# Planner rates, later SSM phase tables and a half output stage in two equal parts, in a fused conformer and SSM step

## The chip, the core and the metric

The kernel runs on one core of a Trainium2 chip. The metric is the device time of one launch in microseconds (us); the median of three runs of the kernel before is 1973.45 us. The engines of the core work side by side and wait for each other by semaphores: TensorE (PE, matrix products, with PEld its weight loads), VectorE (DVE), ScalarE (ACT), GpSimd (POOL), and SyncE (SP), whose queue issues the DMAs.

## The reference

One step of a decoder layer on 2048 prompt tokens and 8 sample tokens, width 1024, all in fp32. A gated causal convolution of 31 taps and a diagonal complex SSM (32 groups of 16 channels and 64 states) run side by side, are merged, projected, and an input embedding is added under a gate. Cut to what matters (only the prompt's names, without the states that are returned):

```
h = rmsnorm(x, g_pre)
proj = h @ w_in                       # 1024 -> c_a, c_b, c_z (1024 each), s_x, s_z (512 each), g_c, g_s (1024 each)
u = c_a * sigmoid(c_b)
v = causal_depthwise_conv(u, 31 taps)
v = silu(layernorm(v)) * silu(c_z)    # mean and variance over the 1024 channels
y_c = v @ w_pc
lb = exp(a*dt) (complex), bb = (lb-1)/a * b
s[t] = lb * s[t-1] + bb @ s_x[t];  ys = Re(c @ s) + d * s_x
ys = gelu(ys); ys = ys * sigmoid(ys @ w_glu + b_glu) * silu(s_z)
m = sigmoid(g_c) * y_c + sigmoid(g_s) * (ys @ w_ps)
x1 = x + rmsnorm(m @ w_out, g_post)
y = x1 + rmsnorm(p @ w_ple, g_ple) * sigmoid(x1 @ w_pg + b_pg)
```

## The kernel before

Channels lie on the 128 partitions and tokens on the free axis. The tokens are worked in two halves: the first has 1032 (1024 of the prompt and the 8 samples), in three blocks of 344; the second 1024, in two of 512. Every matrix product is made of three fp32r products, hi by hi, hi by lo and lo by hi (L288 to L290): operands are split into a rounded part (hh, vh, mh, whi: ScalarE, L338 and L251) and the rest (hl, vl, ml, wlo: VectorE or GpSimd, L331). A weight block is 128 x 1024 (raw, 512 KB). It is fetched by SP's queue into one of two buffers, ScalarE casts it to whi, GpSimd subtracts to wlo in two pieces of 512, and only then is the buffer free again.

One half runs through these stages: the input norm; s_x; the pairs c_b and c_a (u in unit c); g_c; s_z; the SSM's products and w_glu; g_s with w_ps; c_z; w_pc (tiles vh, vl); w_out (tiles mh, ml of m); w_pg (mh, ml of x1). Beside them VectorE runs the convolution, 31 multiply-adds per channel block with the accumulator in PSUM (L183, acc and u), of which some taps are taken by ScalarE and GpSimd instead (cq and ca). Then the LayerNorm: the mean by a product with a matrix of averages (L363 and L364, nh and nl), u minus mean, the squares, the variance by the same product, an inverse square root, and v = silu(...) times cz, split into vh and vl. Before the first SSM product the kernel makes tables in `ssm_setup`: for each of four channel batches b, gt (powers times bb), its transposes on TensorE (L609) and products with c (L619); and the phases rho and ph, which undo and redo the rotation of the complex state so that only a real decay is left to scan. They come in two lots, x = 0 for batches 0 and 1, and x = 1 for 2 and 3, each by doubling from 1 to 128 columns (`spar` and `ph` tiles, L177 and L180).

What is computed is fixed; the order is made by a planner when the kernel is built. Tasks are Python generators that yield the engine and the earliest time of the next piece. `Background` (L24 on) holds a clock for VectorE, ScalarE and GpSimd and one for TensorE; each `stage` adds the cost of its products to TensorE's clock and `pump` lets those tasks go on whose planned time has come. `cV`, `cS`, `cG` give the planned cost of n columns on each engine, `use` adds it, `pick` chooses VectorE or GpSimd. A task that wants TensorE (a "P" task: the transposes, the SSM's and the means' products) goes only when it has been ready for a margin of 1.2 us. Each engine then runs its instructions strictly in the order so made. `room(k)` holds a task until k SBUF units are free. PSUM gives six banks to products (`bank`).

In the output stage of the first half the tokens go in two parts, a with the block of 344 and b with the two others, 688: w_out a, w_out b, w_pg a, w_pg b; each part fetches and splits its weights anew. The norm of o, x1 and the outputs (y tasks: e, sgp) of a part are VectorE operations of 344 or 688 columns. In the same time `next_h` brings in the second half's x (xn) and makes its hh and hl.

## Time and profile before

| what | value |
|---|---|
| three runs | 1972.57, 1973.45, 1979.47 us |
| profiled execution | 1971.99 us, span 1970.2 us |
| TensorE busy | 1918.5 us (97%), 10386 products |
| VectorE busy | 1442.1 us (73%) |
| ScalarE, GpSimd busy | 765.6 us (39%), 784.8 us (40%) |
| TensorE's granted clock, mean | 0.989 |
| chain that ended last | TensorE 85%, issue 4%, VectorE 4%, GpSimd 2% |

The profile is of one execution. Busy times of an engine are shares of the whole span and say little of a stage; what a stage waits for is read from the waits, and where a moment is disputed from the timeline of one engine, whose rows give start, duration, engine, line, operation, output and inputs, and in brackets how long the engine sat idle before and what released it. TensorE's products overlap, so the pace is the distance from one start to the next, or a window's time over its number of products.

### The profile page before, as it was taken

The numbers are of one execution on the slowest core, as the hardware profiler recorded it, in microseconds if no ns is written. First come the engines' busy times: TensorE is split into PE (matmuls) and PEld (weight loads), VectorE is DVE, ScalarE is ACT, GpSimd is POOL, SyncE is SP. The second block draws the span as 40 slices with busy tenths as digits, with TensorE's granted clock in tenths as the row PEclk, the third lists the DMA queues.
The fourth block names the chain that finished last, engine by engine and source line by source line (L and its number), as shares of the span: only waits on it lengthen the run. The fifth ranks groups of instructions, "written<-read, shape, count | busy, mean of one in ns | idle before, by whom it ended". The sixth has DMA issues, their size and how long they took to land.

```text
span 1970.2 us, 26641 instructions
## 1 busy us (share of the span) xinstructions
PE 1918.5 (97%) x10386; PEld 1723.0 (87%) x10386; DVE 1442.1 (73%) x1696; ACT 765.6 (39%) x1276; POOL 784.8 (40%) x573
## 2 busy tenths in 40 slices
PE   8897999999999999999899999999999999999998
PEld 7797999999999999999798788888888888888877
DVE  6889997899899876444884479888589843442686
ACT  7424211227311364254532223444731353223542
POOL 1437623315422223253533222687743222224554
PEclk9998999999999999999899999999999999999999
DMA  8461344542122215342554463212212211422455
GB/s 315 155 203 62 100 133 141 177 144 78 51 83 78 102 50 193 116 142 93 190 197 164 172 200 123 74 60 91 71 48 75 97 67 43 160 107 77 148 189 174
DMA packets 103286, 243.58 MB, mean 124 GB/s; under 512 B 11752, under 2 KB 44648, under 8 KB 103144
## 3 DMA queue, kind: packets, MB, share of 16 engines
q1 hardware_dynamic: 102840, 241.68, 36.2%
q8 instruction: 81, 1.33, 0.3%
q14 instruction: 45, 0.37, 0.1%
q10 hardware_dynamic: 320, 0.20, 0.0%
HBM read 188.17 MB, written 54.62 MB: 123 GB/s over the span
## 4 chain that ended last, share of the span: by engine, by line
PE 85%; issue 4%; DVE 4%; POOL 2%; ACT 1%; DMA 1%; POOLq 0%; ACTq 0%; SPq 0%; DVEq 0%
PE bank L288 27%; PE bank L290 26%; PE bank L289 26%; PE bank L774 2%; POOL wlo L331 1%; PE bank L777 1%; PE bank L719 1%; DMA raw<-in_w 1%; POOL ca L331 1%; DVE sgp L331 1%; DVE o L183 0%; DVE o L331 0%; DVE ml L331 0%; DVE spar L183 0%; PE bank L308 0%
## 5 line engine op out<-in xcount | busy, mean ns | idle before, releaser
L331 POOL TENSOR_TENSOR wlo<-raw,whi 128x512 fp32r<-128x512 f32 x386 | 566.5, 1486 | 1082.2 <-ACT whi L251 1064.5
L288 PE MATMUL bank<-hh,whi 128*128 128x344 f32 (+1 forms) x1888 | 665.9, 353 | 0.9 <-ACT whi L251 0.9
L289 PE MATMUL bank<-hl,whi 128*128 128x344 f32 (+1 forms) x1888 | 659.9, 350 | 6.8 <-DVE hl L331 6.8
L290 PE MATMUL bank<-hh,wlo 128*128 128x344 f32 (+1 forms) x1888 | 661.2, 350 | 1.4 <-POOL wlo L331 1.4
L183 DVE SCALAR_TENSOR_TENSOR acc<-u,prm,acc 128x1024 f32<-128x1024 f32 x412 | 530.5, 1288 | 11.2
L289 PEld LDWEIGHTS bank<-hl,whi 128*128 128x128 f32 x1888 | 356.9, 189 | 39.4 <-DVE hl L331 7.1
L288 PEld LDWEIGHTS bank<-hh,whi 128*128 128x128 f32 x1888 | 356.4, 189 | 36.9 <-ACT whi L251 1.5
L290 PEld LDWEIGHTS bank<-hh,wlo 128*128 128x128 f32 x1888 | 356.8, 189 | 35.6 <-POOL wlo L331 2.4
L251 ACT CAST whi<-raw 128x512 fp32r<-128x512 f32 x388 | 223.9, 619 | 148.5 <-PE bank L289 68.6
L288 PE MATMUL bank<-mh,whi 128*128 128x344 f32 (+1 forms) x640 | 227.4, 355 | 7.7 <-ACT whi L251 5.8
L290 PE MATMUL bank<-mh,wlo 128*128 128x344 f32 (+1 forms) x640 | 227.1, 355 | 5.2 <-POOL wlo L331 5.1
L289 PE MATMUL bank<-ml,whi 128*128 128x344 f32 (+1 forms) x640 | 226.6, 354 | 0.3 <-DVE ml L331 0.3
L331 POOL TENSOR_TENSOR ca<-ca,cq 128x512 f32<-128x512 f32 x104 | 132.2, 1300 | 39.5 <-ACT cq L881 36.1
L288 PEld LDWEIGHTS bank<-mh,whi 128*128 128x128 f32 x640 | 122.6, 192 | 20.8 <-ACT whi L251 7.1
L290 PEld LDWEIGHTS bank<-mh,wlo 128*128 128x128 f32 x640 | 122.7, 192 | 18.9 <-POOL wlo L331 7.8
L289 PEld LDWEIGHTS bank<-ml,whi 128*128 128x128 f32 x640 | 122.5, 191 | 12.3 <-DVE ml L331 1.1
L289 PE MATMUL bank<-vl,whi 128*128 128x344 f32 (+1 forms) x320 | 111.9, 350 | 0.7 <-DVE vl L331 0.7
L288 PE MATMUL bank<-vh,whi 128*128 128x344 f32 (+1 forms) x320 | 112.2, 351 | 0.0
L290 PE MATMUL bank<-vh,wlo 128*128 128x344 f32 (+1 forms) x320 | 112.0, 350 | 0.0
L881 ACT ACTIVATE cq<-u,prm 128x512 f32<-128x512 f32 x104 | 73.4, 722 | 55.0 <-POOL ca L331 45.9
L331 DVE TENSOR_TENSOR oacc<-oacc,sq 128x344 f32<-128x344 f32 (+1 forms) x35 | 30.6, 874 | 79.2 <-ACT sq L1388 78.7
L177 DVE TENSOR_TENSOR gcl<-bank,gcl 128x344 f32<-128x344 f32 (+1 forms) x40 | 23.5, 587 | 65.7 <-PE bank L290 65.7
(213 smaller groups left out, 2447.7 us busy)
## 6 DMA issues: line engine op xcount, KB each, us to landing
raw<-in_w SPq DMA_DIRECT2D x194, 512.0 KB
cq<-cq SPq DMA_DIRECT2D x12, 512.0 KB
e<-e SPq DMA_DIRECT2D x8, 516.0 KB
rt<-e SPq DMA_DIRECT2D x8, 516.0 KB
gc<-gc SPq DMA_DIRECT2D x8, 516.0 KB
m<-gs SPq DMA_DIRECT2D x8, 516.0 KB
gcl<-gc SPq DMA_DIRECT2D x8, 516.0 KB
m2l<-m SPq DMA_DIRECT2D x8, 516.0 KB
```

The lines of the kernel that those rows point to most:

```text
L177: V.tensor_tensor(out=out, in0=a, in1=b, op=op)
L183: V.scalar_tensor_tensor(out=out, in0=a, scalar=s, in1=b, op0=op0, op1=op1)
L251: S.copy(out=hi, in_=t[:, c])
L288: T.matmul(o, hi[:, w], rh[:, c0:c0 + n], start=kt == 0, stop=False)
L289: T.matmul(o, hi[:, w], rl[:, c0:c0 + n], start=False, stop=False)
L290: T.matmul(o, lo[:, w], rh[:, c0:c0 + n], start=False, stop=kt == k - 1)
L331: (V if e == "V" else GP).tensor_tensor(out=out, in0=a, in1=b, op=op)
L719: T.matmul(pvs[rr][half_[i], jj], we[:, g * P + rr * 64:g * P + rr * 64 + 64], U[:, g, 8:8 + ne], start=True, stop=True)
L774: T.matmul(pvs[i][:, jj], TW[:, :, 2 * j + i], U[:, 2 * j + i, o0:136], start=True, stop=False)
L777: T.matmul(pvs[i][:, jj], cq[half_[i], x * 512 + j * P:x * 512 + (j + 1) * P], X[half_[i], x, j, o0:136], start=False, stop=x == 1)
L881: S.activation(out=q[:, h], in_=u[:, k + x * 512:k + x * 512 + 512], func=AF.Identity, scale=w(k))
```

## The change

Four things. The planner's rates: n/930 + 0.1 for VectorE in place of n/960 + 0.08, n/1190 for n/1250 on ScalarE, 0.3 for 0.16 of fixed cost on GpSimd, 0.4375 ns a column and 7 ns for a product of TensorE in place of n/2400 and 3 ns, `pick` to match, and larger costs for the table work. The margin of P tasks is 4.0 us, not 1.2. The phase tables: rho and x = 0 are made after table b = 0, x = 1 after b = 2, and `ssm_batch` fetches its phases only when they are there. The output stage of the first half has two parts of 516 tokens, each in two blocks of 258. Besides, the gelu and ysn tasks wait for one or two free units.

```diff
-                at = max(self.clock[e], r) if e in self.clock else r + (1.2 if e == "P" else 0.0)
+                at = max(self.clock[e], r) if e in self.clock else r + (4.0 if e == "P" else 0.0)
...
-        return "V" if v + n / 960.0 <= g + n / 478.0 + 0.3 else "G"
+        return "V" if v + n / 930.0 <= g + n / 478.0 + 0.4 else "G"
...
-    cV = lambda n: 0.08 + n / 960.0
+    cV = lambda n: 0.1 + n / 930.0
...
-    cS = lambda n: 0.13 + n / 1250.0
-    cG = lambda n: 0.16 + n / 478.0
+    cS = lambda n: 0.13 + n / 1190.0
+    cG = lambda n: 0.3 + n / 478.0
+    cPr = lambda n: 0.007 + n * 0.4375e-3
...
+        OUT_PARTS = [[[(0, 258), (258, 258)], [(516, 258), (774, 258)]], [[(0, 512)], [(512, 512)]]]
...
-                bg.pe += 3 * k * (n / 2400.0 + 0.003)
+                bg.pe += 3 * k * cPr(n)
...
-            r0 = use("V", 5.6, 3.0)
+            r0 = use("V", 11.0, 3.0)
...
-            tt(k1, mag, mag)
...
-            tt(rho, k1, k1)
...
-                unit_length(*ph[0], v2)
...
-            r0 = use("V", 6.5, r0)
-            for x in range(2):
+            def phases(x, r0):
...
-                    r0 = use("V", 2.0 + 6 * cV(4 * m), r0)
+                    r0 = use("V", 4.0 + 6 * m / 120.0, r0)
...
+                tables["phases"] = 2 * x + 2
+                tables["ph", x] = queue["data"] + 1.0
+                return r0
...
+                if b == 0:
...
+                    tt(k1, mag, mag)
...
+                    tt(rho, k1, k1)
...
+                        unit_length(*ph[0], v2)
...
+                    r0 = use("V", 13.0, r0)
+                if b % 2 == 0:
+                    r0 = yield from phases(b // 2, r0)
...
-            phu = alloc(name="sph")
-            rp = dma(out=phu[:, 0:1024], in_=ph_d[b], after=tables[b])
...
-            r = max(r1, rp)
+            while tables["phases"] < b + 1:
+                yield None, bg.now + 1.0
+            yield from room(3)
+            phu = alloc(name="sph")
+            r = max(r1, dma(out=phu[:, 0:1024], in_=ph_d[b], after=tables["ph", b // 2]))
...
+                yield from room(1)
...
+                yield from room(1)
...
-            parts = [[blocks[i] for i in p] for p in PARTS[h]]
+            parts = OUT_PARTS[h]
```

The steps of rho (from `tt(k1, mag, mag)` on) and `phases` stand in `ssm_setup`; `phu`, the tile of the phases, in `ssm_batch`; `room(1)` in `gelu_task`. The lines of the new kernel are numbered 1 to 18 higher (products L290 to L292, transposes L591, means L365 and L366).

First place: TensorE, the first transposes of the table of batch 0 (ident, gt) in the pairs of c_b and c_a. Before, where 720 products with h stand ahead of them:

```order
L288 MATMUL bank<-hh_431,whi 128x344
L289 MATMUL bank<-hl_432,whi 128x344
L290 MATMUL bank<-hh_431,wlo 128x344
L609 MATMUL bank<-ident,gt_2027 128x128 x4
L288 MATMUL bank<-hh_417,whi 128x344
```

Now, with 336 ahead of them:

```order
L290 MATMUL bank<-hh_436,whi 128x344
L291 MATMUL bank<-hl_437,whi 128x344
L292 MATMUL bank<-hh_436,wlo 128x344
L591 MATMUL bank<-ident,gt_1264 128x128 x4
L290 MATMUL bank<-hh_422,whi 128x344
```

The transposes have moved 384 products towards the start.

Second place: VectorE, behind the products that end bb (which gt needs). Before, rho begins here, and gt of batch 0 stands about 200 rows on, behind both lots of phases:

```order
L177 TENSOR_TENSOR bb_729<-bb_729 128x256
L331 TENSOR_TENSOR re_743<-re_743,rt_989 128x1032
L331 TENSOR_TENSOR re_743<-re_743,rt_1102 128x1032
L177 TENSOR_TENSOR spar_727<-spar_727 128x16 x2
L177 TENSOR_TENSOR rho<-spar_727 128x16
```

Now gt is made here, and rho stands behind the first tile of u and the first operation of its convolution (acc<-u,prm):

```order
L178 TENSOR_TENSOR bb_737<-bb_737 128x256
L333 TENSOR_TENSOR re_744<-re_744,rt_989 128x1032
L178 TENSOR_TENSOR gw_1265<-pwr_120,bb_737 128x512
L178 TENSOR_TENSOR gw_1265<-pwr_121,bb_737 128x512
L178 TENSOR_TENSOR gt_1264<-gw_1265 128x512
...
L178 TENSOR_TENSOR u_1379<-bank,sg_1275 128x344 x2
L839 MEMSET u_1379 128x30
...
L181 TENSOR_SCALAR acc<-u_1379,prm 128x1024
L178 TENSOR_TENSOR spar_735<-spar_735 128x16 x2
L178 TENSOR_TENSOR rho<-spar_735 128x16
```

The table goes ahead of the phases, and the phases of x = 0 go behind the work that u brings.

Third place: TensorE, the product that gives the variance (nh, nl with avgr) and the first products of v. Before, 264 products with h stand between them:

```order
L364 MATMUL bank<-nl_6807,avgr 128x344
L288 MATMUL bank<-hh_417,whi 128x344
...
L290 MATMUL bank<-hh_431,wlo 128x344
L288 MATMUL bank<-vh_7014,whi 128x344
L289 MATMUL bank<-vl_7015,whi 128x344
```

Now 120 do:

```order
L366 MATMUL bank<-nl_7010,avgr 128x344
L290 MATMUL bank<-hh_422,whi 128x344
...
L292 MATMUL bank<-hh_436,wlo 128x344
L290 MATMUL bank<-vh_7217,whi 128x344
L291 MATMUL bank<-vl_7218,whi 128x344
```

The mean that comes before the variance has moved by the same 144 products, with 192 products between the two as before.

## Rows read from the trace of the kernel before

**Rows 1.** The page's part 1: busy time, share of the span, instructions.

```profile
PE 1918.5 (97%) x10386; PEld 1723.0 (87%) x10386; DVE 1442.1 (73%) x1696; ACT 765.6 (39%) x1276; POOL 784.8 (40%) x573
```

**Rows 2.** Timeline of TensorE: start, duration, product, count, and in brackets idle before.

```profile
84.09 0.65 PE L289 MATMUL bank<-hl,whi 128*128 128x344 f32 x1 [6.78 <-DVE hl L331]
...
196.17 1.09 PE L609 MATMUL bank<-ident,gt 128*128 128x128 f32 x4 [14.08 <-issue]
```

**Rows 3.** Timeline of VectorE, 105 to 197.

```profile
105.22 0.71 DVE L177 TENSOR_TENSOR spar<-spar 128x16 f32<-128x16 f32 x2
...
192.17 0.69 DVE L177 TENSOR_TENSOR ph<-ph 128x512 f32<-128x512 f32 x1
...
194.06 1.29 DVE L177 TENSOR_TENSOR gw<-pwr,bb 128x512 f32<-128x512 f32 x2
195.38 0.69 DVE L177 TENSOR_TENSOR gt<-gw 128x512 f32<-128x512 f32 x1
```

**Rows 4.** Windows: length, PE, PEld, DVE, ACT, POOL busy (instructions), clock, DMA share, GB/s.

```profile
97.70:142.00 44.30, 44.30 (x282) 44.30 (x282) 36.79 (x136) 13.93 (x26) 19.34 (x25) 1.00 0.63 194
142.00:193.00 51.00, 40.09 (x255) 39.81 (x253) 49.56 (x96) 21.61 (x34) 35.04 (x27) 0.92 0.22 73
193.00:520.00 327.00, 323.41 (x2134) 315.68 (x2135) 298.07 (x340) 106.47 (x200) 118.76 (x89) 0.99 0.38 125
520.00:667.30 147.30, 147.30 (x936) 147.30 (x935) 135.47 (x142) 32.50 (x60) 38.31 (x28) 1.00 0.25 86
```

**Rows 5.** VectorE's groups by form, busy and mean ns: 114.6:141.6, then 152.3:186.6.

```profile
L177 DVE TENSOR_TENSOR ph<-ph,spar 128x8 f32<-128x8 f32 x14 | 2.7, 240 | 0.2
...
L177 DVE TENSOR_TENSOR ph<-ph,spar 128x8 f32<-128x8 f32 x6 | 3.9, 692 | 0.1
```

**Rows 6.** Timeline of GpSimd, 152 to 160.

```profile
152.31 7.58 POOL L331 TENSOR_TENSOR ca<-ca,cq 128x512 f32<-128x512 f32 x6 [0.62 <-ACT cq L881]
```

**Rows 7.** Waits of VectorE, 219 to 668: total us, times, longest.

```profile
DVE u L177 <- PE bank L290: 10.4, 6, 3.0
DVE gs L177 <- PE bank L290: 6.4, 14, 1.6
```

**Rows 8.** Timelines of VectorE, ScalarE and TensorE, 666 to 756.

```profile
666.14 1.28 DVE L183 SCALAR_TENSOR_TENSOR u<-u,prm,acc 128x1024 f32<-128x1024 f32 x1
...
709.61 1.42 ACT L376 ACTIVATE mean<-bank,epsc 128x344 f32<-128x344 f32 x3
...
714.55 1.23 DVE L177 TENSOR_TENSOR acc<-acc,mean 128x1032 f32<-128x1032 f32 x1 [9.14 <-ACT acc L384]
...
754.64 1.23 DVE L331 TENSOR_TENSOR vl<-cz,vh 128x1032 fp32r<-128x1032 f32 x1 [1.12 <-ACT vh L338]
...
755.93 0.43 PE L289 MATMUL bank<-vl,whi 128*128 128x344 f32 x1 [0.71 <-DVE vl L331]
```

**Rows 9.** Windows at the start of w_pg in the first half.

```profile
936.00:978.00 42.00, 35.49 (x200) 33.20 (x199) 32.48 (x32) 23.02 (x37) 22.06 (x14) 0.92 0.56 194
978.00:996.00 18.00, 13.68 (x51) 12.59 (x52) 16.95 (x22) 4.75 (x9) 7.10 (x4) 0.62 0.58 188
```

**Rows 10.** Waits of TensorE, 930 to 1060: total us, times, longest.

```profile
PE bank L288 <- ACT whi L251: 5.3, 3, 3.9
PE bank L290 <- POOL wlo L331: 3.3, 3, 1.7
```

**Rows 11.** Timeline of VectorE, 987 to 990.

```profile
987.58 1.66 DVE L331 TENSOR_TENSOR ml<-o,mh 128x688 fp32r<-128x688 f32 x2 [0.83 <-ACT mh L338]
```

**Rows 12.** A window of products of 512 columns.

```profile
1640.00:1700.00 60.00, 60.00 (x260) 48.57 (x259) 19.88 (x12) 17.37 (x26) 17.29 (x12) 1.00 0.23 79
```

**Rows 13.** Timeline of TensorE, 207 to 209.

```profile
207.24 1.87 PE L619 MATMUL bank<-cbd,gt 128*128 128x32 f32 x16
208.94 0.40 PE L288 MATMUL bank<-hh,whi 128*128 128x344 f32 x1
```

**Rows 14.** Timeline of VectorE, 1061 to 1063.

```profile
1061.29 1.29 DVE L183 SCALAR_TENSOR_TENSOR xn<-xn,prm,rb 128x1024 f32<-128x1024 f32 x1 [9.41 <-DMA xn<-in_xT]
```

More of the change, by code (lines that the diff above doesn't have):

```diff
@@ L309, in stage_pair @@
             w_ahead(wstate["use"], 0)
-            bg.pe += 6 * len(rhs) * sum(n / 2400.0 + 0.003 for _, n in blocks)
+            bg.pe += 6 * len(rhs) * sum(cPr(n) for _, n in blocks)
             bg.pump(pe=False)
@@ L445, in exp_dve @@
             tt(out, q, ki.bitcast(F32))
-        tables = {"done": 0}
+        tables = {"done": 0, "phases": 0}
         def ssm_setup():
@@ L478, in ssm_setup @@
             ts(th, th, -3.1415925, 3.1415925, ALU.max, ALU.min)
-            r0 = use("V", 1.6, r0)
+            r0 = use("V", 2.5, r0)
             yield "S", r0
@@ L504, in ssm_setup @@
             tt(fim, k1, k3)
-            r0 = use("V", 4.0, r0)
+            r0 = use("V", 7.0, r0)
             yield "V", r0
@@ L657, in ssm_setup, with unit_length @@
                 tables[b] = queue["data"] + 1.0
+                if b == 0:
+                    yield "V", r0
+                    tt(k1, mag, mag)
+                    tt(k1, k1, k1)
+                    tt(rho, k1, k1)
+                    ph = [[k1, k2], [k3, nre]]
+                    def unit_length(re, im, t):
+                        tt(t[0], re, re)
+                        tt(t[1], im, im)
+                        tt(t[0], t[0], t[1], ALU.add)
+                        ts(t[0], t[0], -0.5, 1.5)
+                        tt(re, re, t[0])
+                        tt(im, im, t[0])
+                    v2 = [wk[:, x * 16:x * 16 + 16] for x in range(2)]
+                    V.tensor_copy(out=ph[0][0], in_=cs)
+                    V.tensor_copy(out=ph[0][1], in_=sn)
+                    for x in range(3):
+                        unit_length(*ph[0], v2)
+                        cmul(*ph[1], *ph[0], *ph[0], *v2)
+                        ph.reverse()
+                    r0 = use("V", 13.0, r0)
+                if b % 2 == 0:
+                    r0 = yield from phases(b // 2, r0)
             free(bb, bcu, cbd, pu)
@@ L1206, in ysn_task @@
             def ysn_task(b):
+                yield from room(2)
                 yield "S", ready[b]
+                yield from room(2)
                 ysn[b] = hilo("yn")
```

18 lines of the change are left out of this document (1 added, 17 removed).

## The prediction

> **What bounds the kernel now.** I read the page first: TensorE is busy for 1918.5 of 1970.2 us [rows 1], so a change can win only what TensorE still waits, and lose whenever a helper engine comes late. Then the timeline of TensorE in the early part of the first half, for its waits: 14.08 us at L609, the transposes of the first SSM table, and 6.78 us for a lo tile of h [rows 2]. The timeline of VectorE tells where L609's came from: rho and the phase tables begin at 105.22, end at 192.86, and only then is table 0's gt made; its first half is done at 196.07 [rows 3]. The windows of the first half give VectorE's load: busy 36.79 + 49.56 + 298.07 + 135.47 = 519.9 of the 569.6 us from 97.7 to the end of the convolution at 667.3 [rows 4]. It sets the convolution's end, and behind that stands the LayerNorm chain. Then the output stage: in 936 to 996 TensorE issued 200 + 51 products [rows 9]. One of 344 columns takes 147.30 / 936 = 0.157 us [rows 4]; 251 of them make 39.5 us out of 60, so 20.5 us are lost there.
>
> The sum is made against the profiled execution, 1971.99 us (span 1970.2), which lies 1.46 under the median of 1973.45.
>
> **The tables (stall at L609).** In the new order 336 products of the main stage stand before the first transpose, where 720 stood. TensorE reached it at 196.17 - 14.08 = 182.1 [rows 2]; 384 products less are 60.4 us, so now at 121.7. VectorE makes gt where rho's first row stood, from 105.22; six operations take 2 x (1.29 + 0.69) = 4 us by the rows of gt and gw [rows 3]. It is done before 110, so the 14.1 us go. The 6.78 us for hl may go as well: the second mean of the input norm is issued 70 rows earlier on TensorE, yet the same 40 small parameter operations stand before that hl. I take 4 of 6.8, with 0 and 6.8 as bounds.
>
> **What comes late instead.** The 41 rho operations and the x = 0 phases leave an opening in which VectorE had nothing else, and now stand behind the first convolution operation. From 97.7 to 142 VectorE was busy 36.79 us [rows 4], and from 105.22 on nearly all of it is this work; less some 5 us of SiLU additions and u evacuations I count 31; 4 us of gt take its place, so 27 us move past 142. There GpSimd runs ca additions of 1.26 us back to back [rows 6], and an 8-wide product of phases takes 0.69 instead of 0.24 us [rows 5]. In before the x = 1 tables bore this, 51 us (142 to 192.86) where x = 0 took some 27 (36.8 from 105.22 to 142, less rho). Now x = 0 can bear it and x = 1 also.
>
> The Trainium skill (SBUF — State Buffer, section "SBUF: two separate sides") says the port pair that VectorE and GpSimd share is an exclusive lock: an operation of VectorE with two SBUF inputs blocks for a whole GpSimd operation. By that every small operation would pay up to a whole ca; the trace has 0.69 for the 8-wide one, so less than that, and the measurement decides.
>
> Where does it land? First on PSUM: evacuations u<-bank queue behind the phase operations, and TensorE has six banks. No row of before has this wait. From below 0 (VectorE catches up between blocks), from above the 27 us moved; I take 8, as the operations are issued in pieces with evacuations between.
>
> Second on the convolution's end: +27 moved; seven taps fewer on VectorE in this half by the new order, 7 x 1.28 = -9; contention 0 to +24 (51 - 27), I take +12. Against it VectorE waited 10.4 and 6.4 us for TensorE's banks [rows 7], which a late VectorE no longer does: -17. That is 27 - 9 + 12 - 17 = +13. Bounds: with no contention and all 28.9 + 11.8 = 40.7 us idle of 193 to 667.3 [rows 4] absorbed, -23; with full contention and nothing absorbed, +42.
>
> **The LayerNorm.** The new order puts the variance mean 120 products before the first product of v, where 264 stood. In before the variance left PSUM at 709.61, the last vl came at 755.87 and TensorE got its last v tile at 755.93 [rows 8]: 46.3 us, of which 264 + 21 products (44.9 us) covered all but the one short wait. Now 120 + 21 cover 22.2, so about 24 are missing; VectorE idles 9.14 us in that chain for ScalarE's part of the square root [rows 8] and some of its operations were slow, so it can be up to 8 shorter. I take 19 of new wait. TensorE's own path to v is then -14.1 - 4 + 8 + 19 = +9, without the bank waits +1, at best (6.8 won, a wait of 15) -6. VectorE's path is +13. The later one counts: **+13**, bounds -6 to +42. The stall that goes is so handed to the LayerNorm; this is the term that decides.
>
> In the second half hundreds of products stand between the variance and v in both orders, nothing there.
>
> **The output stage of the first half.** 64 weight tiles x 3 products x 2 matrices make 1152 products of 344 columns, and now 1536 of 258. One of 512 columns takes 60.00 / 260 = 0.231 us [rows 12], one of 344 0.1574 [rows 4]; the line through both gives 0.1198 for 258; 1536 x 0.1198 - 1152 x 0.1574 = **+2.7 us**. From below: a 128-column weight load with 32 columns of product repeats in (208.94 - 207.24) / 16 = 0.106 [rows 13], which would be -18.
>
> The waits: TensorE waited there mostly for whi and wlo [rows 10], as a weight block of 24 products was used up in 3.8 us of pg a at 344 columns, while GpSimd then makes its two wlo in 2 x 1.3 at best, and only behind them the raw tile is free for the next transfer. With 516 columns a block lasts 5.7 us. The last lo tiles of x1 of the second part came at 989.2 [rows 11], and without waits the first is needed at 936 + 192 x 0.157 = 966; now it is needed 46 us after the out stage, and the chain has tiles of 516 instead of 688 columns, but 18 e and sgp operations between them. I take **-14** of the 20.5; bounds -21 (all) and -5 (weights still late, the y work contended).
>
> **Start of the second half.** Four xn transfers are now queued behind one raw, where two were; VectorE waited 9.41 us for the first of them [rows 14]. Each further pair xn and hl is 3.5 us of VectorE with its hh between, and TensorE takes a tile every 2.8 us. I take **+3**, from 0 to +10. The planner's rates and the wider margin for P tasks cost nothing by themselves; what they move is in these orders. For what they move elsewhere I allow 3 us either way.
>
> Sum: 13 + 2.7 - 14 + 3 = +4.7; 1971.99 + 4.7 = 1976.7, and with 1.46 for the median **1978**.
>
> **Rivals.**
> 1. VectorE keeps up (faster). For it: 40.7 us of idle on VectorE in 193 to 667; the bank waits that it no longer has. Against: 24 us of missing cover before v. Then -6 to v, -20 in the output stage, +2.7: -23.3, about 1950.
> 2. VectorE loses the convolution (slower). One mechanism: phase operations beside ca, at 0.69 instead of 0.24 us and more for wider ones, hold the engine past the point where the convolution's idle can take it up. Price: +32 to v; the output stage, in the same contention, wins 9 only, +2.7, +6 at the boundary: +31.7, about 2005. It decides once the last tap ends over 19 us later than 667.42 [rows 8]. For it the 51 against 27 us of the two phase tables; against, the spread of x = 1 over a longer stretch.
> 3. Narrow products run at a steeper rate. As a mechanism here: each pays its columns alone. At the 0.106 of the 32-column products, a weight load each, they would give -18 in place of +2.7, about 1957. Against it: the line through two widths of this trace has a fixed part of 7 ns only, so 258 columns alone are 0.113. The Trainium skill (TensorE: Matmul & The Clock Gate, section "Back-to-back issue gap") lists 262 cycles for 256 columns, 0.109 us at 2.4 GHz, which would put the sum near this rival; its 518 cycles for 512 are 0.216 us, and the trace has 0.231.
> 4. They gain nothing from being narrow, 0.157 each: 384 more of them, +60, about 2036. Against it the 0.106 of the 32-column products [rows 13].
>
> **How the numbers follow.** The forecast (two stalls go, the LayerNorm and the boundary take as much back) 0.37, its own range 1964 to 1983; rival 1 0.28, rival 2 0.28, rival 3 0.04, rival 4 0.01, 0.02 for something else. No change means within 0.5%, 9.9 us, about what a measurement of this kernel can tell: 1963.6 to 1983.3. So faster 0.32, same 0.37, slower 0.31. The range leaves out the outer part of rivals 1 and 2: 1952 to 2000.
>
> **What would show it.** Right: no wait at the first transposes; rho and x = 0 on VectorE after 137, at about 1 us an operation; waits of TensorE for u in 140 to 200; the last tap at about 680; a wait for vl L331 of some 15 to 24 us before w_pc; the output stage 14 us shorter. Wrong: a convolution that ends by 667 with no wait for v (rival 1), one past 686 (rival 2), a pitch at 258 columns far from 0.120 (rivals 3 and 4), or a second half that moves by more than 3 us.

## The result, and the profile after

The changed kernel takes 2004.17 us, median of 4 runs (2001.16 to 2005.67), against 1973.01 of the kernel before on the same chip; the ratio is 1.0148, interval 1.0124 to 1.0173. It is slower by 1.5%, outside the forecast's range and at the time of rival 2. The profiled span is 1999.4 us, 29.2 more than before.

Page of the changed kernel, part 1, to be read beside [rows 1]:

```profile
PE 1932.0 (97%) x10772; PEld 1731.2 (87%) x10772; DVE 1458.8 (73%) x1690; ACT 785.1 (39%) x1324; POOL 829.6 (41%) x596
```

The shares tell nothing of it. Where the time went is read from TensorE's windows between points that both kernels have: first product with h, first product of y (the s branch, yh), first of v (vh), first of w_out, first of the second half. Windows of before (length, busy PE, PEld, DVE, ACT, POOL, granted clock, DMA):

```profile
56.70:499.80 443.10, 420.10 (x2727) 411.08 (x2726) 404.01 (x642) 150.93 (x277) 186.82 (x163) 0.97 0.40 131
499.80:751.60 251.80, 251.80 (x1599) 251.80 (x1598) 215.32 (x207) 93.65 (x148) 72.15 (x47) 1.00 0.21 71
751.60:843.70 92.10, 91.39 (x578) 91.10 (x577) 48.00 (x75) 25.81 (x45) 24.49 (x16) 1.00 0.44 162
843.70:1048.30 204.60, 193.59 (x1164) 189.38 (x1163) 131.88 (x139) 95.72 (x174) 97.35 (x64) 0.95 0.49 165
```

The same stretches of the changed kernel:

```profile
59.10:497.50 438.40, 421.52 (x2721) 411.54 (x2720) 376.83 (x589) 149.87 (x280) 213.44 (x179) 0.98 0.41 131
497.50:756.40 258.90, 254.74 (x1604) 254.07 (x1603) 234.86 (x232) 92.10 (x148) 72.07 (x48) 0.99 0.23 74
756.40:866.10 109.70, 98.22 (x583) 93.88 (x582) 71.06 (x94) 41.54 (x61) 25.20 (x16) 0.92 0.40 140
866.10:1061.50 195.40, 189.75 (x1545) 188.60 (x1545) 116.03 (x136) 91.14 (x190) 98.59 (x64) 0.98 0.49 161
```

The number of products in each of the first three stretches is the same within missing records, so the lengths can be subtracted: start +2.4, h to y -4.7, y to v +7.1, v to w_out +17.6 (w_out starts 22.4 later, 866.1 against 843.7), output stage -9.2, second half 937.9 against 921.9, +16.0. That is the 29.2.

**The stall at the first transposes is gone, and others stand in its place.** TensorE's timeline of the changed kernel, against [rows 2]:

```profile
113.87 0.60 PE L591 MATMUL bank<-ident,gt 128*128 128x128 f32 x4
...
160.00 1.63 PE L726 MATMUL bank<-U,swe 128*64 128x136 f32 x12 [3.88 <-DVE u L178]
...
219.69 0.93 PE L591 MATMUL bank<-ident,gt 128*128 128x128 f32 x4 [4.94 <-DVE gt L178]
```

No wait at the first table, 4.94 us at the second, 3.88 for u at the first SSM product. The waits of TensorE between 90 and 560 (total, times, longest):

```profile
PE bank L290 <- DVE u L178: 5.1, 1, 5.1
PE bank L591 <- DVE gt L178: 4.9, 1, 4.9
PE bank L292 <- POOL wlo L333: 4.5, 4, 3.5
PE bank L726 <- DVE u L178: 3.9, 1, 3.9
```

**VectorE.** Its timeline against [rows 3]:

```profile
97.82 1.66 DVE L178 TENSOR_TENSOR gt<-gw 128x512 f32<-128x512 f32 x1
...
133.80 0.37 DVE L178 TENSOR_TENSOR spar<-spar 128x16 f32<-128x16 f32 x2
...
143.66 7.98 DVE L178 TENSOR_TENSOR spar<-spar 128x16 f32<-128x16 f32 x11
```

and GpSimd beside it, as in [rows 6]:

```profile
147.79 7.58 POOL L333 TENSOR_TENSOR ca<-ca,cq 128x512 f32<-128x512 f32 x6
```

rho begins at 133.8 instead of 105.22, and eleven of its 16-wide operations take 7.98 us, 0.73 each, beside GpSimd's work; the same eleven took 3.73 before. These means hide two prices. The eleven one by one (shortest, median and longest in ns, first and last start), in the changed kernel and then in before:

```profile
L178 DVE TENSOR_TENSOR spar<-spar x11: 161/1145/1318, 143.7 to 150.5; 128x16 f32<-128x16 f32 x11
...
L177 DVE TENSOR_TENSOR spar<-spar x11: 163/175/1153, 107.5 to 111.0; 128x16 f32<-128x16 f32 x11
```

An operation takes 0.16 to 0.18 us, or 1.15 to 1.32 us, and each of the long ones ends 0.03 us behind the end of a GpSimd operation (an addition to ca or a wlo, 1.3 us each). Six of the eleven are held in this way now, two were in before. The windows of [rows 4], the last one up to the new last tap:

```profile
97.70:142.00 44.30, 44.09 (x287) 43.77 (x287) 19.92 (x37) 16.80 (x29) 29.79 (x28) 1.00 0.74 224
142.00:193.00 51.00, 46.06 (x287) 44.80 (x286) 49.28 (x101) 23.46 (x44) 39.67 (x32) 0.90 0.13 36
193.00:520.00 327.00, 316.14 (x2059) 308.38 (x2058) 293.76 (x385) 99.87 (x187) 125.48 (x90) 0.98 0.37 120
520.00:695.30 175.30, 171.14 (x1072) 170.47 (x1072) 171.73 (x181) 47.99 (x82) 47.38 (x33) 0.98 0.27 90
```

VectorE idles 24.4 us in the first window (7.5 before), and its busy time up to the last tap is 534.7 us, 14.8 more than in [rows 4].

**The LayerNorm.** VectorE, then TensorE, against [rows 8]:

```profile
694.01 1.28 DVE L184 SCALAR_TENSOR_TENSOR u<-u,prm,acc 128x1024 f32<-128x1024 f32 x1
...
697.77 1.23 DVE L333 TENSOR_TENSOR nl<-acc,nh 128x1032 fp32r<-128x1032 f32 x1 [1.12 <-ACT nh L340]
...
707.13 6.92 DVE L333 TENSOR_TENSOR u<-u,mean 128x1032 f32<-128x1032 f32 x5 [7.00 <-ACT mean L376]
...
742.13 1.23 DVE L178 TENSOR_TENSOR acc<-acc,mean 128x1032 f32<-128x1032 f32 x1 [10.18 <-ACT acc L386]
...
775.38 1.23 DVE L333 TENSOR_TENSOR vl<-cz,vh 128x1032 fp32r<-128x1032 f32 x1 [1.12 <-ACT vh L340]
```

```profile
705.41 0.32 PE L365 MATMUL bank<-nh,avgr 128*128 128x344 f32 x1
...
736.59 0.32 PE L365 MATMUL bank<-nh,avgr 128*128 128x344 f32 x1
...
775.40 0.65 PE L290 MATMUL bank<-vh,whi 128*128 128x344 f32 x1 [1.49 <-ACT vh L340]
776.66 0.65 PE L291 MATMUL bank<-vl,whi 128*128 128x344 f32 x1 [0.61 <-DVE vl L333]
777.12 0.49 PE L292 MATMUL bank<-vh,wlo 128*128 128x344 f32 x1
777.40 0.49 PE L290 MATMUL bank<-vh,whi 128*128 128x344 f32 x1
```

The last tap ends at 695.3 (667.4 before). nl of the mean is ready at 699.0, but its products come at 705.41, without a wait: that is their place in TensorE's order. VectorE is the one that sits idle, 7.00 us, for the mean. From 756.4 on each block of v comes one by one, and the last two rows show the second loss there: products that wait for nothing start 0.28 us apart, not 0.157. That is the clock, by the window of these rows:

```profile
777.00:779.00 2.00, 2.00 (x8) 2.00 (x8) 1.33 (x2) 0.00 (x0) 1.98 (x2) 0.50 0.00 0
```

A granted clock of 0.50 is the lower of the two levels, 1.2 GHz. It fell while TensorE waited for one tile of v after the other (0.71 in 761 to 765), and from 781 on it is 1.00 again.

**The output stage.** Window of products of 258 columns, and the window of the stall that is left:

```profile
880.00:930.00 50.00, 50.00 (x415) 49.89 (x414) 14.34 (x23) 23.96 (x56) 23.80 (x18) 1.00 0.35 112
...
1008.00:1019.00 11.00, 7.39 (x38) 6.88 (x37) 9.08 (x10) 4.27 (x9) 6.53 (x4) 0.69 0.46 146
```

50.00 / 415 = 0.1205 us. In 1008 to 1019 some 38 products take 11 us, 6.4 too many; two more are lost at 942. In [rows 9] it was 20.5.

**The second half.** The eight scans of the SSM's third batch in before:

```profile
1192.44 3.10 DVE L750 TENSOR_TENSOR_SCAN sc<-rho,sfin,sc 128x128 f32<-128x128 f32 x8
```

and in the changed kernel, VectorE, then GpSimd:

```profile
1233.17 9.17 DVE L761 TENSOR_TENSOR_SCAN sc<-rho,sfin,sc 128x128 f32<-128x128 f32 x8
```

```profile
1227.52 6.93 POOL L333 TENSOR_TENSOR ca<-ca,cq 128x512 f32<-128x512 f32 x4
...
1237.91 9.00 POOL L333 TENSOR_TENSOR ca<-ca,cq 128x512 f32<-128x512 f32 x6
```

They come 41 us later (13 of them because the half starts later), fall into a row of ca additions, and take three times as long. TensorE then waits for them:

```profile
PE bank L788 <- DVE sc L178: 5.0, 3, 2.6
```

From the half's first product to the first of y it takes 408.3 us, 398.4 before.

### The profile page after: what moved, and what is told of

Its sections match the earlier page's. It is cut to its first block, busy times and chain, and to the rows that moved or that the text cites. A ratio compares the mean times of both kernels' runs of the same rounds, so it can differ in the third digit from the quotient of the medians.

```text
span 1999.4 us, 27491 instructions
## 1 busy us (share of the span) xinstructions
PE 1932.0 (97%) x10772; PEld 1731.2 (87%) x10772; DVE 1458.8 (73%) x1690; ACT 785.1 (39%) x1324; POOL 829.6 (41%) x596
## 4 chain that ended last, share of the span: by engine, by line
PE 61%; issue 5%; DVE 5%; POOL 3%; DMA 1%; ACT 0%; POOLq 0%; SPq 0%; DVEq 0%
PE bank L292 20%; PE bank L290 20%; PE bank L291 20%; POOL wlo L333 2%; DVE acc L184 1%; DVE sc L761 1%; DMA raw<-in_w 1%; PE bank L785 1%; DVE sc L178 1%; DVE stmq L178 0%; PE bank L788 0%; DVE stmp L178 0%; DVE vl L333 0%; POOL yl L333 0%; DVE cz L333 0%
## 5 line engine op out<-in xcount | busy, mean ns | idle before, releaser
L290 PE MATMUL bank<-hh,whi 128*128 128x344 f32 (+1 forms) x1888 | 666.4, 353 | 6.8 <-DVE u L178 5.1
L292 PE MATMUL bank<-hh,wlo 128*128 128x344 f32 (+1 forms) x1888 | 662.9, 351 | 6.4 <-POOL wlo L333 6.4
L290 PEld LDWEIGHTS bank<-hh,whi 128*128 128x128 f32 x1888 | 358.2, 190 | 44.0 <-DVE u L178 5.4
L292 PEld LDWEIGHTS bank<-hh,wlo 128*128 128x128 f32 x1888 | 358.1, 190 | 40.3 <-POOL wlo L333 8.3
L290 PE MATMUL bank<-mh,whi 128*128 128x258 f32 (+1 forms) x768 | 248.3, 323 | 5.8 <-ACT whi L253 5.8
L292 PE MATMUL bank<-mh,wlo 128*128 128x258 f32 (+1 forms) x768 | 248.4, 323 | 5.4 <-POOL wlo L333 5.3
L291 PE MATMUL bank<-ml,whi 128*128 128x258 f32 (+1 forms) x768 | 247.7, 323 | 0.0
L333 POOL TENSOR_TENSOR ca<-ca,cq 128x512 f32<-128x512 f32 x124 | 166.0, 1368 | 30.6 <-ACT cq L892 30.6
L292 PEld LDWEIGHTS bank<-mh,wlo 128*128 128x128 f32 x768 | 146.6, 191 | 18.8 <-POOL wlo L333 7.4
L290 PEld LDWEIGHTS bank<-mh,whi 128*128 128x128 f32 x768 | 146.8, 191 | 18.0 <-ACT whi L253 6.7
L291 PEld LDWEIGHTS bank<-ml,whi 128*128 128x128 f32 x768 | 146.5, 191 | 11.8 <-DVE ml L333 0.4
L290 PE MATMUL bank<-vh,whi 128*128 128x344 f32 (+1 forms) x320 | 113.3, 354 | 5.7 <-ACT vh L340 5.7
L892 ACT ACTIVATE cq<-u,prm 128x512 f32<-128x512 f32 x124 | 87.8, 722 | 75.0 <-POOL ca L333 58.3
L292 PE MATMUL bank<-vh,wlo 128*128 128x344 f32 (+1 forms) x320 | 112.9, 353 | 0.0
L333 DVE TENSOR_TENSOR oacc<-oacc,sq 128x258 f32<-128x258 f32 (+1 forms) x42 | 30.1, 725 | 94.7 <-ACT sq L1403 94.6
L291 PEld LDWEIGHTS bank<-vl,whi 128*128 128x128 f32 x320 | 61.0, 191 | 14.1 <-DVE vl L333 8.3
```

Source lines behind the costliest of these rows:

```text
L290: T.matmul(o, hi[:, w], rh[:, c0:c0 + n], start=kt == 0, stop=False)
L291: T.matmul(o, hi[:, w], rl[:, c0:c0 + n], start=False, stop=False)
L292: T.matmul(o, lo[:, w], rh[:, c0:c0 + n], start=False, stop=kt == k - 1)
L333: (V if e == "V" else GP).tensor_tensor(out=out, in0=a, in1=b, op=op)
L892: S.activation(out=q[:, h], in_=u[:, k + x * 512:k + x * 512 + 512], func=AF.Identity, scale=w(k))
```

## The experiments

Each was timed beside the kernel before; times are medians, and the ratios are to it. The table has the stretches of each profile as above, "cover" for the products with h between variance and v, and the last column for the second half. A is the kernel before, B the changed one.

| kernel | us | h to y | y to v | cover | v to w_out | w_out at | out stage | last tap | 2nd half |
|---|---|---|---|---|---|---|---|---|---|
| before | 1973.0 | 443.1 | 251.8 | 264 | 92.1 | 843.7 | 204.6 | 667.4 | 921.9 |
| changed | 2004.2 | 438.4 | 258.9 | 120 | 109.7 | 866.1 | 195.4 | 695.3 | 937.9 |
| only_tables | 2006.9 | 454.8 | 251.6 | 168 | 102.6 | 867.8 | 203.4 | 698.7 | 934.1 |
| only_rates | 1984.0 | 426.7 | 252.1 | 144 | 105.7 | 848.4 | 208.2 | 684.7 | 927.2 |
| only_parts | 1963.4 | 448.9 | 251.8 | 264 | 92.1 | 850.1 | 190.6 | 673.8 | 923.5 |
| only_margin | 2075.3 | 525.8 | 255.1 | 408 | 92.8 | 930.6 | 209.3 | 728.3 | 934.9 |
| new_tables_in_opening | 2061.1 | 500.4 | 257.2 | 120 | 109.9 | 925.4 | 195.2 | 753.8 | 937.9 |
| new_x0_in_opening | 2007.7 | 449.8 | 251.4 | 120 | 110.1 | 869.5 | 195.5 | 699.7 | 939.2 |
| new_margin_1_2 | 2005.2 | 464.8 | 252.1 | 168 | 102.0 | 882.4 | 190.7 | 712.2 | 930.6 |
| new_old_rates | 2010.5 | 458.5 | 252.5 | 168 | 102.7 | 873.3 | 194.2 | 693.9 | 942.1 |
| new_early_sph | 2007.3 | 440.2 | 258.3 | 120 | 110.1 | 867.5 | 195.7 | 696.3 | 942.7 |
| new_h2_margin | 1995.2 | 437.3 | 259.2 | 120 | 110.9 | 864.7 | 196.8 | 692.7 | 932.4 |
| new_half_taps | 1994.1 | 434.1 | 253.6 | 120 | 111.1 | 856.8 | 197.0 | 684.6 | 938.0 |
| new_means_earlier | 1995.3 | 438.4 | 261.1 | 192 | 99.1 | 857.0 | 196.4 | 694.5 | 937.3 |
| old_parts_gt_first | 1977.6 | 425.9 | 255.2 | 96 | 111.2 | 849.9 | 189.5 | 684.5 | 937.7 |
| parts_gt_only | 1971.6 | 432.7 | 254.2 | 96 | 111.4 | 856.1 | 190.9 | 685.6 | 922.8 |
| parts_tables_early_sph | 1966.1 | 426.0 | 255.2 | 96 | 111.1 | 849.6 | 190.2 | 684.2 | 926.1 |
| tables_means_earlier | 1962.0 | 426.1 | 253.6 | 120 | 110.2 | 848.5 | 189.6 | 685.7 | 922.8 |
| parts_half_taps | 1960.3 | 443.4 | 251.8 | 264 | 92.1 | 845.8 | 192.1 | 669.5 | 922.6 |
| parts_side6 | 1967.0 | 442.2 | 255.7 | 288 | 91.8 | 847.3 | 191.7 | 670.0 | 928.8 |

### One part of the change alone

**only_tables**: A, with rho and the phases made behind tables b = 0 and b = 2, later phases, and the rooms.

```diff
-            for x in range(2):
+            def phases(x, r0):
...
+                if b % 2 == 0:
+                    r0 = yield from phases(b // 2, r0)
```

> The kernel before with the later phase tables alone (rates, margin and output parts as before). Theory 1 (the phase operations, moved beside GpSimd's ca additions, delay the end of the convolution and with it v): the 14 us stall at the first transposes is gone, the last tap ends at 680 to 695 instead of 667, and the time is 8 to 22 us longer than before. Theory 2 (the planner's new rates and margin place the means and the SSM's products badly): the stall goes and nothing comes back, 5 to 14 us shorter, the last tap at 670 or earlier.

Ratio 1.0163 [1.0148, 1.0178]: the tables alone cost as much as all four parts together, more than either theory had. The last tap is late as in theory 1, at 698.7.

**only_rates**: A with the new costs of `cV`, `cS`, `cG`, `cPr` and `pick`.

```diff
-    cV = lambda n: 0.08 + n / 960.0
+    cV = lambda n: 0.1 + n / 930.0
```

> The kernel before with the planner's new rates alone. Theory 1: the order moves a little, time within 6 us of before, the convolution ends within 8 us of 667. Theory 2: the variance mean stands near 120 products before v instead of 264, a wait of 10 to 20 us for v, time 10 to 25 us longer, also a few us lost in the second half's SSM.

Ratio 1.0046 [1.003, 1.0062]. The stall at the transposes goes by the plan alone (h to y -16.4), the cover too (v to w_out +13.6). That is theory 2's loss at v, with less of a price in all since the stall goes.

**only_parts**: A with two parts of 516 tokens.

```diff
-            parts = [[blocks[i] for i in p] for p in PARTS[h]]
+            parts = OUT_PARTS[h]
```

> The kernel before with the two equal output parts alone. Both theories: the stage from w_out to the second half is 8 to 12 us shorter, the 258-column products are paced at 0.120 us, time 1961 to 1966. If the narrow parts only move the weight waits, within 3 us of before.

Ratio 0.9941 [0.9924, 0.9957], in the expected range. The output stage is 14.0 shorter, more than expected, and most of it is kept.

**only_margin**: A with the wider margin.

```diff
-                ... r + (1.2 if e == "P" else 0.0)
+                ... r + (4.0 if e == "P" else 0.0)
```

> The kernel before with the margin of 4.0 us for products of tasks alone. Theory 1: within 4 us of before. Theory 2: the SSM's and means' products come later in TensorE's order, 5 to 15 us longer, with the loss before v or in the second half's SSM.

Ratio 1.0509 [1.049, 1.0528], far outside both theories. The largest waits of TensorE from 90 to 600:

```profile
PE bank L777 <- DVE sc L177: 48.0, 1, 48.0
PE bank L609 <- DVE gt L177: 12.6, 1, 12.6
```

One product of the last SSM batch stands 48 us ahead of its input. By their ratios the four alone come to +32 + 9 - 12 + 100 us; made together, the four cost +29. They act on one plan and can't be added.

### Parts taken back

**new_margin_1_2** and **new_old_rates**: B with the margin of 1.2, and B with the old rates.

```diff
-                at = ... (4.0 if e == "P" else 0.0)
+                at = ... (1.2 if e == "P" else 0.0)
```

> The changed kernel with the old margin of 1.2 us. By the run of the margin alone (101 us slower, 48 of it one wait for batch 3's sc) the margin hurts where a batch comes late; theory 1: here the tables set VectorE's end, so within 8 us of the changed kernel, the last tap at 690 to 700. Theory 2: 10 to 25 us faster than the changed kernel, 1979 to 1994, with 168 instead of 120 products behind the variance and a shorter wait for v.

> The changed kernel with the old rates. Theory 1: the last tap stays late (690 or later) and the time is 2000 or more; as the old plan takes the table work for shorter than it is, more waits for gt and sc, up to 2060. Theory 2: 168 products behind the variance, time 5 to 15 us under the changed kernel's.

Ratios 1.0163 [1.0148, 1.0178] and 1.0188 [1.0172, 1.0203]: with the tables late neither matters much, as theory 1 has it for both, but with the margin of 1.2 the last tap comes at 712.2, outside its range. The smaller margin makes the second half 7.3 and the output stage 4.7 shorter, and w_out 16.3 later.

**new_tables_in_opening** and **new_x0_in_opening**: B with rho and x = 0 ahead of TensorE's first transposes, right behind gt; in the first x = 1 as well, in the second x = 1 stays at b = 2.

```diff
+                if b == 0:
+                    tt(k1, mag, mag)
...
+                    r0 = use("V", 13.0, r0)
+                    r0 = yield from phases(0, r0)
```

> The changed kernel, but rho and both phase lots stand straight behind the first gt, ahead of u (gt of batch 0 stays first); rates, margin and parts as changed. Theory 1 (the phases' place, beside ca and behind u, costs VectorE the convolution): no stall at the first transposes, the last tap at 665 to 678 instead of 695, the wait for v shorter, 12 to 25 us faster than the changed kernel, 1980 to 1992. Theory 2 (the order of means and SSM products by rates and margin costs the time): the last tap moves but v still waits about 18 us, since 120 products stand behind the variance, and the time stays within 6 us of the changed kernel's 2004.

> The changed kernel with rho and x = 0 straight behind the first gt, x = 1 behind table 2 as changed (the run with x = 1 ahead of table 1 too lost 61 us to one wait for batch 3's sc). If VectorE's lateness in the convolution sets the time: rho and x = 0 take 37 us again instead of some 75, the last tap at 670 to 685, 8 to 20 us faster than the changed kernel. If the tables' place on TensorE (products of the SSM later) costs as much: a new wait for sc or gt before yh, within 5 us of 2004 or slower.

Ratios 1.0447 [1.0431, 1.0462] and 1.0174 [1.0158, 1.0189]. In the first TensorE waits for one product as only_margin does:

```profile
PE bank L789 <- DVE sc L178: 61.2, 1, 61.2
```

The time is neither theory's. In the second rho, spar and ph take 62 us in all their rows, where the changed kernel's take 100. Not all of this is taken off VectorE: its busy time up to the last tap is 524.3 us, 10.4 less, since seven more taps stand on it (9 us) and the SSM's scans, beside GpSimd now, take 28.6 us instead of 19.3. The last tap does not come earlier (699.7). But the run has a new wait, as its second theory said; the largest of TensorE from 90 to 700, and of VectorE up to 700:

```profile
PE bank L789 <- DVE sc L178: 14.4, 1, 14.4
...
DVE u L178 <- PE bank L292: 41.6, 12, 7.7
```

VectorE's waits for banks of u all lie before 411, where it is ahead of TensorE; then TensorE waits 14.4 us for scans of which eight take 10.98 us, and h to y is 11.4 us longer than in the changed kernel. So the run does not tell what contention in the convolution costs by itself: what the move gave back there, if anything, stands against this wait.

**new_early_sph**: B with the second half's phases fetched beside swe, ahead of the U products, as before.

```diff
+            if not first:
+                phu = alloc(name="sph")
+                rp = dma(out=phu[:, 0:1024], in_=ph_d[b], after=tables["ph", b // 2])
```

> The changed kernel, but in the second half each SSM batch fetches its phases (sph) beside its swe, as before, not behind its U products. The first half's order is unchanged. If the late fetch pushes the second half's scans into the time in which GpSimd adds ca: the scans take 0.46 us each again, no wait for sc at L788, 7 to 12 us faster than the changed kernel, 1992 to 1997. If the second half lost its time to the margin and the rates: within 3 us of 2004.

Ratio 1.0174 [1.0159, 1.0189]: no gain, and the third batch's scans of the second half take 10.21 us. **new_h2_margin** does the same and has the margin of 1.2 in the second half:

```diff
+            if h:
+                bg.margin = 1.2
```

> The changed kernel with two of its edits taken back in the second half only: the phases are fetched with swe, before the U products, and the margin of P tasks is 1.2 us. Theory A (late phases and wide margin each push the second half's SSM to where GpSimd's ca runs, and one is enough): alone each gave nothing (942.7 us with early phases, 930.6 with the margin of 1.2 everywhere, 937.9 changed), together the second half takes 920 to 930 us and the time is 1988 to 1996. Theory B (the second half is late for another reason, such as the planner's rates): 935 to 943 us and within 4 us of 2004.

Ratio 1.0115 [1.01, 1.013], in theory A's range; the second half is 5.5 shorter, between the two theories. Its eight scans take 3.11 us. But new_margin_1_2, with late phases, has 3.11 too: in the changed kernel the margin decides, not the fetch. In kernels at old rates and margin it is the fetch, see below.

### The tables' order on the kernel with two parts

**old_parts_gt_first**: only_parts with gt first, x = 0 behind table 0, x = 1 behind table 1, phases fetched late. **parts_gt_only**: only_parts with no more than gt of batch 0 ahead of rho. **parts_tables_early_sph**: old_parts_gt_first with the early fetch.

```diff
+            first_gt = yield from make_gt(0, max(r0, r1))
...
+                gt, wt, r1 = (yield from make_gt(b, r1)) if b else first_gt
```

> The kernel before with the two equal output parts, with gt of batch 0 ahead of rho and the x = 0 phases (x = 1 behind table 1). The 14 us stall at the transposes goes without work moved behind u. If VectorE's convolution decides when v comes, the gain is taken back as a wait for v: within 4 us of 1963. If the stall is lost time by itself: 1948 to 1954. A mean placed late on TensorE (96 products to v) would make it slower than 1967.

> The kernel before with two equal output parts and gt of batch 0 ahead of rho; both lots of phases follow at their old place, sph early in the second half. The stall at the transposes goes with nothing moved behind u. Handed on: 96 products stand behind the variance, v waits 15 to 25 us, time 1960 to 1970. Not handed on: 1946 to 1952.

> The run with the old parts replaced and gt first (1977.6), with sph early in the second half. By the late-fetch explanation the second half is 8 to 13 us shorter, 1964 to 1970; the first half is unchanged (w_out from 850).

Ratios 1.0025 [1.0015, 1.0036], 0.9992 [0.9983, 1.0001] and 0.9962 [0.9947, 0.9976]. y comes 16 to 23 us earlier than in only_parts, since the transposes wait no more; v to w_out takes 19 longer, and w_out starts between 0.5 earlier and 6 later. So the gain is handed on to v each time. The fetch is worth 11.6 us of second half here, as expected: 937.7 against 926.1.

### VectorE's load or TensorE's order

**new_half_taps** and **parts_half_taps**: B and only_parts with six taps of each channel block of the first half at 512 columns, which leaves out part of the convolution.

```diff
+                    if h == 0 and k in (2, 3, 4, 5, 6, 7):
+                        stt(acc[:, 0:512], u[:, k:k + 512], w(k), acc[:, 0:512], ALU.mult, ALU.add)
```

> The changed kernel, but in the first half six of the 31 taps of each channel block (k = 2 to 7) are worked on 512 of their 1024 columns only; the order of instructions is the same on every engine. This leaves out part of the convolution. A tap of 1024 columns is 1.28 us and one of 512 about 0.69, so some 48 taps shorter by 0.59 give VectorE 28 us less work before the last tap. Theory A (VectorE's convolution sets when v and w_out start): the last tap ends 20 to 28 us earlier, at 667 to 675 instead of 695.3, w_out starts at 842 to 850 instead of 866.1, and the time is 1978 to 1988. Theory B (the lateness comes from what TensorE and the planned order hand to VectorE, which then waits instead): VectorE's idle time grows by what the taps save, the last tap stays within 6 us of 695 and the time within 8 us of 2004.

> The kernel before with the two equal parts alone (1963.4 us), with the same six taps of each channel block on 512 of 1024 columns in the first half; this leaves out part of the convolution. Its w_out starts at 850.1 us, its last tap ends at 673.8. Theory A (VectorE's convolution sets the start of w_out here too): the last tap 15 to 28 us earlier, w_out at 828 to 838, time 1944 to 1953. Theory B (with the old tables TensorE's own products set the start): the last tap earlier, but w_out within 5 us of 850 and the time 1959 to 1967.

Ratios 1.0111 [1.0094, 1.0128] and 0.9938 [0.9923, 0.9953]. In new_half_taps neither theory has it. VectorE up to the last tap in new_half_taps (the changed kernel had 534.69 of 597.60):

```profile
97.70:684.60 586.90, 572.51 (x3692) 562.62 (x3693) 507.91 (x700) 188.07 (x339) 242.77 (x182) 0.99 0.35 114
```

27 us less work bring the last tap 10.7 and w_out 9.3 earlier, and 16 us more idle time. The time from v to w_out does not shrink (111.1). What shrinks are TensorE's waits before v (y to v 253.6, h to y 434.1). The longest wait for u goes from 5.1 to 0.9, those for wlo together from 5.3 to 3.3. So VectorE's load counts in the changed kernel, by way of TensorE's waits. In parts_half_taps 27 us less work, too, move w_out by 4.3 (theory B), which stands in h to y, where single runs differ by as much; apart from hl and the first transposes (6.7 and 14.1 us in both runs) TensorE waits for VectorE little there, 3.2 us for sc in only_parts.

**new_means_earlier** and **tables_means_earlier**: B, and parts_tables_early_sph, with the two LayerNorm products of the first half taken earlier in TensorE's order, 48 and 72 products in the one, 24 in the other.

```diff
-            yield "P", ready
+            yield "P", ready - early
...
+                (mean,), r = yield from mean_task(acc, blocks, None, r, 1, True, 0.0 if h else 6.0)
```

> The changed kernel, but in the first half TensorE's order has the LayerNorm's mean 48 products earlier and the variance 72 earlier, so that 192 products, not 120, stand between the variance and the first of v; nothing else is changed in the sources. In the changed kernel nl of the mean was ready at about 699 and its product came at 705.4, nl of the variance at 732 and its product at 736.6. Theory A (the place of the two products in TensorE's order sets v: in all kernels with less cover than 264 the start of w_out came 128.5 to 130.2 us behind the variance): mean at 699, variance at about 727, w_out at 855 to 857 instead of 866.1, the wait at v 17.6 us shrinks to about 7, time 1992 to 1996. Theory B (VectorE's convolution, which ends at 695, and the work behind it set v): the two products wait as much longer for nl, w_out stays within 3 us of 866 and the time within 5 us of 2004.

> The kernel with the two parts, the tables' new order and the phases of the second half fetched early, at old rates and margin (1966.1 us), with mean and variance of the first half's LayerNorm 24 products earlier in TensorE's order (120 between variance and v, not 96). Its mean's nl was ready at 688 and the product came at 692.2. Theory A: variance and w_out 3 to 4 us earlier (w_out at 845 to 846, not 848.9), time 1961 to 1964. Theory B: the same within 1.5 us.

Ratios 1.0114 [1.0099, 1.0129] and 0.9948 [0.9931, 0.9965]. TensorE's rows of the mean and the variance in new_means_earlier:

```profile
698.28 0.42 PE L366 MATMUL bank<-nl,avgr 128*128 128x344 f32 x1 [0.85 <-DVE nl L333]
...
726.75 0.43 PE L366 MATMUL bank<-nl,avgr 128*128 128x344 f32 x1 [0.83 <-DVE nl L333]
```

The last tap stays (694.5), w_out comes 9.1 earlier, the kernel is 8.9 faster. That is theory A: moving two sets of six products did it. Now they wait a little for nl, so VectorE is the next bound, 9 us behind, and w_out is still 13.3 later than in before. At v TensorE now waits 4.6 us for the wlo of its first weights. GpSimd makes the two pieces beside VectorE's operations of 1032 columns for v, which follow each other without a gap:

```profile
747.82 17.34 POOL L333 TENSOR_TENSOR wlo<-raw,whi 128x512 fp32r<-128x512 f32 x2 [7.70 <-ACT whi L253]
```

In the changed kernel the two take 3.69. The last vl comes at 768.5, so without the wlo TensorE would have waited about as long for v. In tables_means_earlier, counted from the first product with h, the two came 3.8 earlier and w_out 2.5; the second half is 3.3 shorter, too, which the move does not explain.

**parts_side6**: only_parts, where GpSimd may take taps while six units are free.

```diff
-                if units.left() >= 8:
+                if units.left() >= 6:
```

> The kernel before with the two equal parts alone (1963.4 us), and GpSimd may take taps of the convolution while six SBUF units are free, not eight: 31 additions to ca of 512 columns in the first half where there were 23, and 288 products with h between the variance and v, not 264. Theory A (VectorE's convolution sets v's start, any tap taken off it counts): 8 more additions are 4 taps of 1.28 us, the last tap ends 3 to 5 us earlier, w_out too, 1957 to 1961. Theory B (the taps that GpSimd takes hold VectorE up by as much through the shared SBUF, or v already waits for the LayerNorm chain): 1962 to 1968.

Ratio 0.9974 [0.9964, 0.9983], in theory B's range: w_out 2.8 earlier, the second half 5.3 longer.

only_parts (1963.4) and tables_means_earlier (1962.0) beat both kernels; they were not run side by side, and their 1.4 us are within what their runs differ by.

## Why the prediction was wrong, step by step

Against +4.7 in the sum the profile has +29.2. Of the 24.5 us between them 9.4 lie before w_out (+22.4, not +13), 13.0 behind the output stage (+16.0, not +3), and 2.1 in the output stage. So two steps failed: TensorE's own path to v, and the second half, which was put at nothing.

- **The stall at L609**: right. It is gone, and nearly all of the wait for hl with it, not 4 us only: at the start of the products with h about 1.4 us are lost where it was 11.7 in before, counted over the pace of 0.157.
- **Waits for u, +8**: right in size. 5.1 + 3.9 = 9.0.
- **19 us of new wait at v**: right. v to w_out is 17.6 longer. In every kernel here with a cover of 192 or less, w_out starts 128.5 to 130.2 us behind the last of the variance products, however many products stand between; with 264 it is 133.9, and TensorE waits hardly at all. So the chain behind the variance needs about 129 us, and cover beyond what hides it buys nothing.
- **TensorE's own path to v, +9: the first step that failed.** It measured +22.4. The sum held the right waits but took the way to v as free of others. It left out the second table's gt (4.9 us), wlo at 531 to 540 (y to v +7.1), a start 2.4 later, and the lower clock level behind the waits (the granted clock is 0.90 in 142 to 193, a window that also holds the 3.9 for u). h to y won 4.7, where -10 was counted. The two paths are not apart, either: u and gt, for which TensorE waits here, are VectorE's, and of the 9.3 us that new_half_taps won some 4 are the wait for u.
- **VectorE's path, +13**: the last tap came 27.9 late. The seven taps less, 9 us, are there. Idle time in the opening was 17 us more, not 27; contention cost some 24, not 12 (the largest, each summed over its rows: rho and spar 13, the copies usm and tails 5, scans 4, ph 3, re 2); and of the 17 us that idle time was to absorb it took 4. But in the changed kernel it does not decide alone: nl was ready 6.4 us before TensorE asked. Taking the later of the two paths gave +13 for v; what sets it is the place of two products on TensorE, for 9 of the 22.4 us (new_means_earlier). In the 13.3 that are left the products wait for nl; the runs do not separate what VectorE's own load has in these and what its waits for TensorE have.
- **Rival 2** gave the right time, about 2005, in part by luck. Its sign came (the last tap past 686), and so did its contention. But it put +32 to v, where +22.4 came, 9 of them due to the place of two products, with the contention left as it was; and the 14.5 us of the second half, of which it has nothing, fill its sum up. How much of the other 13.3 is contention stays open: new_x0_in_opening loses 14.4 us to another wait.
- **The exclusive lock.** By the Trainium skill (SBUF — State Buffer, section "SBUF: two separate sides") whichever of the two operations, VectorE's with two SBUF inputs or GpSimd's, starts first has the shared pair for the whole instruction, and the other fully blocks. The trace agrees: 0.16 to 0.18 us for a 16-wide product that runs free, 1.15 to 1.32 for one that is held until a GpSimd operation ends. The prediction took a mean, 0.69, for a size of its own and the rule for refuted; 0.69 and 0.73 are mixtures of the two prices, and what changes is how many operations are held.
- **258 columns**: right. 0.1205 us against 0.1198; rivals 3 and 4 fall.
- **Output stage**: -11.3 forecast with the pace, -9.2 measured; 9 us of wait are left where 6.5 were expected. Alone it is -14.0.
- **Boundary, +3**: the h pair of the second half takes 26.6 us, 25.1 before.
- **Second half, "nothing there": the second step that failed**, 14.5 us beside the boundary. It looked at the LayerNorm alone. 8.4 are the SSM: in the nine kernels whose third batch has its eight scans in 9.2 to 11.2 us, the way from the half's first product to y takes 408 to 414 us; in the others, with 3.1 to 5.1, it takes 398 to 403. The rest is in the last stage, w_out and w_pg, 6.3 longer: 193.3 to 195.4 us in all kernels whose margin there is 4.0, 186.6 to 191.6 with 1.2. How the margin does that was not taken apart; the listed waits are for whi and wlo, 5.4 us in all, 2.2 in before, and behind the longest the granted clock is 0.50 (1941 to 1947).

Why the two products stood so late is the planner's doing: only_rates has a cover of 144, only_tables 168, only_margin 408. Which cost in the plan makes it was not tried.

## What to carry to other kernels

In a kernel whose engines run a fixed order, a stall that is removed early shows up again at the next place where the order was made for the old timing; so follow the last wait of the stage, and count how many products cover it. Before blaming the engine that makes a late input, see if its consumer was there to ask: an input ready 6 us before its product points at the order, and moving that product is a cheaper trial than taking load off the producer. Here it won 9 us, about that slack at the two products, and then the producer was the next bound. Small operations that move in time change their price, by what the engine next to them does at the new time; read them one by one, since a mean can mix two prices. And a run that moves work to take one cost away needs its own list of waits before it counts as a test of that cost.

## What the runs showed of the hardware that was not expected

- Eight scans of 128 x 128 take 3.10 us alone and 9.2 to 11.2 beside GpSimd's additions and wlo. One by one a scan takes 0.45 us or about 1.45, and one of the 16-wide products above 0.16 to 0.18 or 1.15 to 1.32; the long ones end with a GpSimd operation.
- It goes the other way, too: in new_means_earlier two wlo pieces of GpSimd take 17.34 us beside a row of VectorE's operations of 1032 columns, 3.69 in the changed kernel. TensorE then waits for them.
- Some of what a wait costs stands in the rows behind it: after a chain of short waits TensorE's products of 344 columns start 0.28 us apart, not 0.157, though nothing is waited for, at a granted clock of 0.50 (777 to 779).
